# A fixed matmul order through the attention stages of a fused encoder layer, and forget gates summed by a scan

## The chip, the cores and the metric

The kernel runs on one core of a Trainium2 chip. The core has five engines that work side by side, each through its own queue in order: TensorE (PE; matmuls, with a weight load, PEld, ahead of each), VectorE (DVE), ScalarE (ACT), GpSimd (POOL) and SyncE (SP, which here only issues DMAs). They wait for each other through semaphores. The metric is the device time of one execution in microseconds (us), taken as the median of several runs.

## The reference: what is computed

One layer of a streaming encoder on 512 tokens of 1024 channels, all in float32.

- `h = RMSNorm(x)` feeds one input projection of 5640 columns, and four branches take their parts of it: A, differential attention (4 heads, each with two 64-wide halves whose softmaxes are subtracted), F, forgetting attention (8 heads of 64), C, a gated convolution with 31 taps, and D, a short gated convolution with 3 taps.
- Branch F adds a bias to its scores: `c = cumsum(log_sigmoid(f_g + b))` along the tokens, and score `(q, k)` gets `c[q] - c[k]` under a causal mask. `f_g` has 8 columns, one for each head.
- Each branch is projected to 1024 channels and multiplied by `sigmoid(h @ w_gate + b_gate)`; the four are summed and projected once more (`w_out`).
- Then cross-attention into 256 memory tokens, and a gated MLP (2816 wide) with a 3-tap convolution. Each of the three parts is added to the residual after an RMSNorm.

## The kernel before

**Products in three passes.** A float32 number is split into a high part in the engine's fast float32 format and a low part (`split`, `load_weights`), and a product is three matmuls (`mm3`): high by high, high by low, low by high. `load_weights` gives each block of weights a DMA on SP into `wr` (2 buffers), a cast on ACT into `wh` (L129), and a subtraction on DVE into `wl` (L130).

**Blocks.** All the heavy work is a list of jobs. `run_blocks` loads weights two jobs ahead, then runs a job's body and calls `bg.tick()`. A body usually runs `channel_major`: 128 output channels by 512 tokens, summed over 8 slices of the input, 24 matmuls of 512 columns. Its PSUM bank comes from a set of four with the tag `mm`; two more banks have the tag `sc` (attention scores), two the tag `tr` (transposes).

**Background tasks.** Everything else is written as generators held by `bg`. Each `yield cost, wait` gives the step's cost on the other engines and how long the step after it is to be held back. `bg.clock` counts the time of the matmuls emitted so far, 0.42 ns for a column and 0.107 us for a transpose. `tick` spends a credit of 0.7 us for each us of that clock on the first two tasks in the queue, as soon as a task's wait is over. In `channel_major` there is a tick after the fourth of eight slices.

**The attention tasks.** For each A head, `qk_jobs` makes two blocks, q (L490 copies on ACT, L491 subtractions on DVE) and k (L498, L499, L500), into a tile `qk` with 2 buffers; then `a_task` has six steps. Step s (0 to 3) does the scores of 128 queries against (s+1)*128 keys, for both halves, into two `sc` banks; DVE adds the mask and takes the row maximum (L557); ACT takes the exponentials (L562); DVE the reciprocals; ACT scales one half (L566), and DVE subtracts the halves (L567). Step s+1 begins with the transposes of that result (`to_keys_major`), whose split goes to `pt` tiles, and steps 3 and 5 multiply them with v (`values`). `f_task` does the same for a pair of F heads; POOL builds the biases (L718, L720) from rows `ck` and columns `cq` of the cumulative gates.

**Order of the stages.** C blocks, D blocks, gates of D, `v_jobs` (v of branch A), q and k of the four A heads, gates of C, `vf_jobs` (v of branch F and the 8 gate columns), q and k of the F pairs mixed with the gates of A, gates of F (`last_branch_jobs`), `w_out`, cross-attention, MLP. `vf_jobs` ends with `forget_gates`: the 8 columns of all tokens go through 9 small DVE and 2 small ACT operations (L647 to L659), then through matmuls with a triangle of ones (L669, `tri`, built by POOL), which sum along the tokens; ACT scales the sums (L670), POOL writes them to DRAM (`crows`, read back by `f_task` as `ck`), and four transposes of 8 rows make `cq`.

**Who sets the order on an engine.** The program is given to a scheduler, which puts the instructions on each engine by the order in which they were emitted and by its own model of when each is ready. On TensorE, a matmul that is emitted early but not ready by that model is passed by later ones that are ready. What it puts in a queue stays in that order on the chip.

## Time and profile before

| | us |
|---|---|
| median of three runs (1113.37 to 1114.11) | 1113.88 |
| the profiled execution's own time | 1114.43 |
| span of its trace, first to last instruction | 1112.7 |
| PE busy in the span | 1093.3 |
| DVE busy | 690.7 |
| ACT busy | 465.6 |
| POOL busy | 107.0 |

By the trace the attention of branch A lies at about 224 to 330 us, the gates of branch C end at about 366 us, the v products of branch F and the forget gates lie at 366 to 407 us, the attention of branch F at 400 to 545 us, the cross-attention at 640 to 760 us, and the MLP fills the rest.

How to read the lines: the page's part 1 gives each engine's busy time; part 2 cuts the span in 40 slices and gives the busy share of each in tenths, with the clock that TensorE was granted (`PEclk`). Groups and waits name an engine, the tile that it writes and a line of the kernel (`PE ps_tr L170` is a transpose); after an arrow stands what released it. A table by windows gives the busy time of each engine in a stretch of time, with the number of its instructions in brackets. Matmuls are pipelined: one of 512 columns is shown with 0.39 us, but the next starts 0.231 us after it, so TensorE can be shown as busy while it waits a little.

### The profile page before, as it was taken

How to read it: one execution, taken by the hardware profiler on the slowest of the kernel's cores; microseconds unless marked ns; L12 is line 12 of the kernel's file. 1: busy time of each engine (PE TensorE's matmuls, PEld its weight loads, DVE VectorE, ACT ScalarE, POOL GpSimd, SP SyncE). 2: the span in 40 equal slices, each digit the busy share in tenths (PEclk: the TensorE clock that was granted, in tenths of full speed). 3: DMA queues.
4: the chain of work that ended last, by engine and by line, in shares of the span. 5: the costliest groups of instructions: out<-in, count | busy, mean ns of one | idle time of the engine just before them, and what ended most of it. 6: DMA issues, size and time to landing. Idle time of an engine off the chain costs nothing.

```text
span 1112.7 us, 14146 instructions
## 1 busy us (share of the span) xinstructions
PE 1093.3 (98%) x5419; PEld 913.1 (82%) x5419; DVE 690.7 (62%) x1123; ACT 465.6 (42%) x783; POOL 107.0 (10%) x199
## 2 busy tenths in 40 slices
PE   7999999999999999999999999999999999999997
PEld 6888888887878978888888889888888888888886
DVE  4899985457565357766464477677666666642224
ACT  4322222467564255555443255445444444431112
POOL 4000001000101024323010130120000000000001
PEclk9999999999999999999999999999999999999999
DMA  6433432331212233333252252333333333332222
GB/s 188 112 92 96 106 90 88 94 95 57 76 59 77 77 115 95 95 95 85 87 189 96 94 171 96 95 95 106 97 97 97 95 96 95 95 95 95 95 76 76
DMA packets 147896, 109.29 MB, mean 98 GB/s; under 512 B 3647, under 2 KB 135340, under 8 KB 147829
## 3 DMA queue, kind: packets, MB, share of 16 engines
q1 hardware_dynamic: 145269, 99.85, 30.2%
q0 software_dynamic: 2560, 8.54, 2.8%
q8 instruction: 43, 0.70, 0.3%
q14 instruction: 24, 0.20, 0.1%
HBM read 106.27 MB, written 2.11 MB: 97 GB/s over the span
## 4 chain that ended last, share of the span: by engine, by line
PE 92%; DVE 2%; DMA 2%; ACT 1%; issue 1%; POOL 1%; SPq 0%; POOLq 0%; DVEq 0%; ACTq 0%
PE ps_mm L166 80%; PE ps_sc L166 7%; PE ps_tr L166 3%; PE ps_tr L170 3%; DVE wl L130 1%; DMA wr<-in_w_in 1%; DMA wr<-in_w_xo 1%; POOL st_r L195 1%; DVE res L890 1%; ACT wh L129 0%; DMA wr<-in_w_xkv 0%; DMA wr<-in_w_xq 0%; DVE htl L110 0%; PE ps_sc L669 0%; DVE e L557 0%
## 5 line engine op out<-in xcount | busy, mean ns | idle before, releaser
L166 PE MATMUL ps_mm<-hth,wh 128*128 128x512 f32 (+1 forms) x984 | 373.1, 380 | 3.0 <-ACT hth L109 1.7
L166 PE MATMUL ps_mm<-htl,wh 128*128 128x512 f32 (+1 forms) x984 | 372.5, 379 | 0.3 <-DVE htl L110 0.3
L166 PE MATMUL ps_mm<-hth,wl 128*128 128x512 f32 (+1 forms) x984 | 372.2, 379 | 0.0
L130 DVE TENSOR_TENSOR wl<-wr,wh 128x1024 fp32r<-128x1024 f32 (+1 forms) x180 | 221.2, 1230 | 235.5 <-ACT wh L129 231.9
L129 ACT CAST wh<-wr 128x1024 fp32r<-128x1024 f32 (+1 forms) x182 | 190.9, 1049 | 374.8 <-PE ps_mm L166 225.8
L166 PEld LDWEIGHTS ps_mm<-hth,wh 128*128 128x128 f32 x984 | 185.7, 189 | 37.5 <-ACT hth L109 1.9
L166 PEld LDWEIGHTS ps_mm<-htl,wh 128*128 128x128 f32 x984 | 185.9, 189 | 35.0 <-DVE htl L110 0.5
L166 PEld LDWEIGHTS ps_mm<-hth,wl 128*128 128x128 f32 x984 | 185.5, 189 | 35.2 <-issue 0.2
L393 DVE SCALAR_TENSOR_TENSOR y<-y,par,y 128x482 f32<-128x482 f32 (+25 forms) x120 | 82.6, 730 | 0.2
L166 PE MATMUL ps_mm<-y,wh 128*128 128x512 f32 x256 | 80.9, 395 | 0.0
L330 DVE SCALAR_TENSOR_TENSOR c<-ps_mm,par,c 128x510 f32<-128x510 f32 x84 | 62.7, 746 | 1.4
L166 PEld LDWEIGHTS ps_mm<-y,wh 128*128 128x128 f32 x256 | 47.5, 188 | 9.9
L166 PE MATMUL ps_mm<-y,wl 128*128 128x512 f32 x128 | 50.8, 397 | 0.0
L192 POOL TENSOR_SCALAR st_m<-pm 128x1 f32<-128x1 f32 x12 | 2.6, 219 | 459.2 <-ACT junk L1142 349.1
L109 ACT CAST acth<-c 128x512 fp32r<-128x512 f32 x22 | 13.6, 620 | 54.7 <-DVE c L1089 54.7
L718 POOL TENSOR_SCALAR fbias<-ck,cq 128x128 f32<-128x128 f32 (+3 forms) x32 | 29.0, 909 | 70.7 <-DVE st L724 65.9
L166 PE MATMUL ps_mm<-wh,actl 128*128 128x512 f32 x88 | 34.6, 393 | 0.0
L166 PE MATMUL ps_mm<-wl,acth 128*128 128x512 f32 x88 | 34.6, 393 | 0.0
L166 PE MATMUL ps_mm<-wh,acth 128*128 128x512 f32 x88 | 34.2, 392 | 0.0
L1083 ACT ACTIVATE c<-ps_mm,par 128x512 f32<-128x512 f32 x42 | 32.4, 772 | 0.0
L109 ACT CAST pth<-ps_tr 128x512 fp32r<-128x512 f32 (+3 forms) x56 | 23.5, 450 | 20.5 <-PE ps_tr L170 19.5
L166 PE MATMUL ps_sc<-qk 128*128 128x128 f32 (+3 forms) x128 | 29.9, 331 | 1.0 <-DVE st L557 0.9
(268 smaller groups left out, 1574.7 us busy)
## 6 DMA issues: line engine op xcount, KB each, us to landing
wr<-in_w_up SPq DMA_DIRECT2D x44, 512.0 KB
wr<-in_w_in SPq DMA_DIRECT2D x40, 512.0 KB
wr<-in_w_gate SPq DMA_DIRECT2D x32, 512.0 KB
wr<-in_w_down SPq DMA_DIRECT2D x22, 512.0 KB
wr<-in_w_branch SPq DMA_DIRECT2D x16, 512.0 KB
wr<-in_w_out SPq DMA_DIRECT2D x8, 512.0 KB
wr<-in_w_xkv SPq DMA_DIRECT2D x8, 512.0 KB
wr<-in_w_in SPq DMA_DIRECT2D x4, 520.0 KB
```

Source lines behind the costliest of these rows:

```text
L109: A.copy(hi, ps)
L129: A.copy(hi[:, :n], raw[:, :n])
L130: low.tensor_tensor(lo[:, :n], raw[:, :n], hi[:, :n].bitcast(F32), ALU.subtract)
L166: PE.matmul(ps, lhs, rhs, start=start, stop=stop)
L170: PE.transpose(ps, x, ident[:n, :n])
L192: G.tensor_scalar(m, parts[0], EPS, None, ALU.add)
L195: G.tensor_tensor(r, m, nhalf[:, :n], ALU.pow)
L330: V.scalar_tensor_tensor(dst[:, s:], src[:, :S - s], w(k), dst[:, s:], ALU.mult, ALU.add)
L393: V.scalar_tensor_tensor(dst[:, s:], src[:, :S - s], pc("conv_dw", k * 4 + j), dst[:, s:], ALU.mult, ALU.add)
L718: G.tensor_scalar(bias[:, :w], ck[j][:, :w], -1.0, cq[:, qt, head:head + 1], ALU.mult, ALU.add)
L890: V.scalar_tensor_tensor(ns.out[t], scaled, rstd_of(ns.work, ms), src, ALU.mult, ALU.add)
L1083: A.activation(c[:, i], ps, AF.Identity, bias=pc("fb", ch), scale=pc("fdw2", ch))
```

## The change

- In the stages from `v_jobs` to the end of branch F's attention (`keep_order(True)` to `keep_order(False)`), every matmul and every transpose is tied to the one emitted before it (`in_order`), so that TensorE runs them in the emitted order.
- `channel_major` calls `bg.tick()` after each slice but the last, no longer only after the fourth. The clock counts 0.45 ns a column and 0.109 us a transpose. After a step that emitted work on TensorE, no task but the bulk ones (the convolution) may start another step for 1.5 us (`gap`, `free`). Both attention tasks get an extra wait at their start, and each step its own wait in place of one for all.
- The gates' sum: the 8 gate columns are transposed (four transposes into an `sc` bank), ACT scales them, and DVE sums them along the 512 tokens with `tensor_tensor_scan` on 8 partitions. The triangle and its matmuls go.
- The first two gate blocks of branch F's output are emitted ahead of `drain("f")`, no longer behind it.

```diff
-    def __init__(self, rate, width):
+    def __init__(self, rate, width, gap):
...
     def step(self, task):
+        start = self.clock
...
         task[2] = self.clock + wait
+        if self.clock > start:
+            self.free = self.clock + self.gap
         return cost
...
-            while self.credit > 0 and task in self.queue and task[2] <= self.clock:
+            while (self.credit > 0 and task in self.queue
+                   and max(task[2], 0.0 if task[3] else self.free) <= self.clock):
                 self.credit -= self.step(task)
...
-    bg = Background(0.7, 2)
+    bg = Background(0.7, 2, 1.5)
...
+    pe_order = SimpleNamespace(kept=False, last=None)
+
+    def in_order(ins):
+        if pe_order.kept and pe_order.last is not None:
+            tc.add_manual_dep(ins.ins, pe_order.last.name,
+                              mybir.DependencyInfo(mybir.DependencyClass.NoSync, mybir.DependencyReason.DATA),
+                              reason="the order of the tensor engine")
+        pe_order.last = ins.ins
+
+    def keep_order(kept):
+        return None, None, lambda: setattr(pe_order, "kept", kept)
+
     def matmul(ps, lhs, rhs, start, stop):
-        PE.matmul(ps, lhs, rhs, start=start, stop=stop)
-        bg.clock += max(int(math.prod(rhs.shape[1:])), 256) * 0.00042
+        in_order(PE.matmul(ps, lhs, rhs, start=start, stop=stop))
+        bg.clock += max(int(math.prod(rhs.shape[1:])), 256) * 0.00045
...
     def transpose(ps, x, n=P):
-        PE.transpose(ps, x, ident[:n, :n])
-        bg.clock += 0.107
+        in_order(PE.transpose(ps, x, ident[:n, :n]))
+        bg.clock += 0.109
...
-            if k == 3 < nk - 1:
+            if k < nk - 1:
                 bg.tick()
...
     def a_task(h, qk, v):
         es, pt, av = {}, None, None
+        yield 0.0, 4.0
...
-            yield cost, 3.5
+            yield cost, (5.0, 5.5, 6.5, 7.5, 3.0, 2.0)[step]
...
-        tri = m1p.tile([P, S], F32, tag="fbias", name="tri", bufs=2)
-        G.memset(tri, 1.0)
-        G.affine_select(out=tri, in_=tri, pattern=[[1, S]], compare_op=ALU.is_ge, fill=0.0, base=0,
-                        channel_multiplier=-1)
         row = e4()
-        pc_ = bank("sc")
+        rz = e4()
+        G.memset(rz[:8, 1], 1.0)
+        pz = bank("sc")
         for kt in range(NT):
-            n = S - kt * P
-            PE.matmul(pc_[:8, kt * P:], z[:, kt], tri[:, :n], start=kt == 0, stop=kt == NT - 1)
-        A.mul(row[:8, 0], pc_[:8, :], HD ** 0.5)
+            transpose(pz[:8, kt * P:(kt + 1) * P], z[:, kt])
+        A.mul(rz[:8, 0], pz[:8, :], HD ** 0.5)
+        V.tensor_tensor_scan(row[:8, 0], rz[:8, 1], rz[:8, 0], 0.0, ALU.mult, ALU.add)
         G.dma_start(crows, row[:8, 0])
...
     def f_task(p, qk, v):
         f_steps[p] = 0
+        yield 0.0, 3.0
...
-            yield cost, 4.5
+            yield cost, (5.0, 5.5, 6.3, 7.2, 2.5, 2.0)[step]
...
+    gf = gate_blocks(1, "f", lambda m: split(acc[m], ns.mix[0][:, m], ns.mix[1][:, m], 0.5))
+
     def mixer_jobs():
...
         yield then(lambda: y.pop("d"))
+        yield keep_order(True)
         yield from v_jobs(O_AV, va)
...
+        yield from itertools.islice(gf, 2)
         yield then(lambda: bg.drain("f"))
+        yield keep_order(False)
...
     def last_branch_jobs():
         yield then(open_last_branch)
-        yield from gate_blocks(1, "f", lambda m: split(acc[m], ns.mix[0][:, m], ns.mix[1][:, m], 0.5))
+        yield from gf
```

More of the change, by code (lines that the diff above doesn't have):

```diff
@@ L8 @@
+import itertools
 import math
@@ L44, with add @@
 class Background:
-    def __init__(self, rate, width):
-        self.queue, self.rate, self.width = [], rate, width
-        self.clock = self.last = self.credit = 0.0
-    def add(self, gen, name):
-        self.queue.append([name, gen, 0.0])
+    def __init__(self, rate, width, gap):
+        self.queue, self.rate, self.width, self.gap = [], rate, width, gap
+        self.clock = self.last = self.credit = self.free = 0.0
+    def add(self, gen, name, bulk=False):
+        self.queue.append([name, gen, 0.0, bulk])
     def step(self, task):
+        start = self.clock
         try:
@@ L345, in done @@
             V.scalar_tensor_tensor(conv_u[:, j], e[:, 1], 1.0, e[:, 0], ALU.add, ALU.mult)
-            bg.add(conv_task(j), "conv")
+            bg.add(conv_task(j), "conv", True)
         for i in range(8):
```

## The prediction

> **What bounds the kernel now.** The page comes first: busy shares, slices, and the chain that ended last.

> ```profile
> PE 1093.3 (98%) x5419; PEld 913.1 (82%) x5419; DVE 690.7 (62%) x1123; ACT 465.6 (42%) x783; POOL 107.0 (10%) x199
> ...
> PE   7999999999999999999999999999999999999997
> ...
> PEclk9999999999999999999999999999999999999999
> ...
> PE 92%; DVE 2%; DMA 2%; ACT 1%; issue 1%; POOL 1%; SPq 0%; POOLq 0%; DVEq 0%; ACTq 0%
> ```

> TensorE is the bound, so the change can gain only what TensorE loses between matmuls, and it loses whatever it makes TensorE wait. A busy share hides short losses. I therefore went through TensorE's order and gave each matmul the spacing of its kind from the timeline (0.231 us for 512 columns, 0.175, 0.118 and 0.066 for 384, 256 and 128, 0.109 for a transpose), and compared with the clock. 20 to 224 us: nothing lost. 224 to 330 (attention A): 106.0 us for 96.8 us of work, 9.2 lost. 330 to 400: 0.7. 400 to 545 (attention F, the same kinds of steps): 2.8. 640 to 760 (cross-attention): 5.9. The rest: nothing. The windows show the same from outside:

> ```profile
> core 0: us, PE busy (x) PEld busy (x) DVE busy (x) ACT busy (x) POOL busy (x), PEclk, DMA share, GB/s
> 224.00:330.00 106.00, 102.86 (x495) 83.60 (x494) 69.72 (x179) 64.74 (x139) 6.04 (x10) 0.98 0.25 73
> 400.00:545.00 145.00, 145.00 (x733) 120.69 (x732) 95.54 (x221) 77.60 (x160) 45.95 (x79) 1.00 0.32 96
> 250.00:253.39 3.39, 2.00 (x11) 1.27 (x11) 3.35 (x13) 1.63 (x5) 0.00 (x0) 1.00 0.09 14
> 253.39:256.80 3.41, 3.41 (x11) 2.36 (x11) 2.96 (x11) 3.39 (x13) 1.04 (x2) 0.50 0.42 142
> 256.80:260.00 3.20, 3.20 (x15) 2.60 (x14) 2.60 (x6) 2.47 (x6) 0.00 (x0) 1.00 0.00 0
> ```

> The reader is to see 3.1 us of open idle time in A and none in F, and that 1.39 us of idle time (250 to 253.39) was followed by 3.41 us at half the granted clock, in which 512-column matmuls start 0.425 us apart. F's loss, 2.1 us without the gates' part, is the floor of such steps; scaled to 106 us it is 1.5. So order and spacing can win back at most 9.2 - 1.5 = 7.6 us.

> The third view is the timeline of DVE and ACT around the forget gates. TensorE's last v matmul started at 388.55, and TensorE went straight on with the next block:

> ```profile
> 390.27 0.42 DVE L110 TENSOR_TENSOR v<-ps_mm,v 128x256 fp32r<-128x256 f32 x1
> ...
> 392.54 0.19 DVE L647 TENSOR_TENSOR fz<-fz_raw,bfg 128x32 f32<-128x32 f32 x1
> ...
> 395.95 0.19 DVE L659 TENSOR_TENSOR fz<-fz,fd 128x32 f32<-128x32 f32 x1
> ...
> 389.89 1.05 ACT L129 CAST wh<-wr 128x1024 fp32r<-128x1024 f32 x1
> ...
> 393.24 1.28 ACT L652 ACT_TABLE_LOAD   x1
> ...
> 402.07 0.59 ACT L670 ACTIVATE e<-ps_sc 8x512 f32<-8x512 f32 x1 [1.21 <-PE ps_sc L669]
> ...
> 399.38 0.40 PE L166 MATMUL ps_mm<-htl,wh 128*128 128x512 f32 x1
> 399.71 2.32 PE L669 MATMUL ps_sc<-tri,fz 128*8 128x512 f32 x8
> 401.96 0.51 PE L166 MATMUL ps_mm<-hth,wl 128*128 128x512 f32 x1
> ```

> The chain through the gates took 3.60 us (392.54 to 396.14), and TensorE did other work for 11 us before it read the result.

> **The change, part by part.**

> *Forget gates.* Before, the eight triangle matmuls held TensorE from 399.61, where the next block matmul was due, to 401.96, plus 0.12 on the matmul behind them; the four row transposes took 0.43 (406.90 to 407.56, less 0.23): 2.9 us. Now both groups of transposes are emitted directly behind the last v matmul, and the order is kept. In the built order of the changed kernel nothing stands between: v matmul, four transposes of the gates, four of the summed rows, then the first q block of branch F. TensorE waits for the whole chain. From the start of the last v matmul: its result at 0.28; on ACT the copy of the third v bank, then a weight cast that is released by that last matmul (1.05), then the last copy (0.37); on DVE the weight subtraction that needs the cast (1.23), the last v subtraction and the gate columns' copy, to 3.1; the chain 3.6, to 6.7; transposes 0.1 + 3 x 0.109 + 0.27, to 7.4; ACT's scale with a hop 0.65, to 8.1; the scan; a hop and the four row transposes 0.45. No row shows a scan. Operations on 512 columns took 0.48 (L733) to 0.75 (L567), twice the dearest would be 1.5; I take 0.75, the row with two tensor inputs. First block matmul at 9.4, in place of 0.12: 9.3 lost (8.3 if the cast and subtraction do not stand in front, 10.5 at the long ends). Net 9.3 - 2.9 = **+6.4** (5.4 to 7.6). Behind the waiting transposes stands all of TensorE's queue, and behind it every engine.
> [...]

> *The clock after that pause.* Six of those 9.3 us are without a matmul, more than the 1.39 that was followed by half clock. In 3.41 us at half clock, 3.41 x (1 - 0.231/0.425) = 1.6 us is lost. Nothing (the half clock falls into the pause) to 3.1 (two such stretches); I take **+1.6**.
> [...]

> *Attention A.* The 7.6 go, and new waits come. By the built order I counted TensorE's work between a step's scores and the transposes of its result: 5.5 to 8.5 us. Against this stands the chain of the step with what the queues of ACT and DVE put before it. Head 0, second step: spacing 5.54; a cast that TensorE releases 1.4 after the scores (1.05), two exponentials 1.4, two k copies 1.2, L566 0.5, L567 0.48: 6.0, late by 0.5. Head 0, last step: spacing 8.2; two q copies, a cast, four k copies, a split, four exponentials, L566 and L567 add up by their rows to 9.5, and with a hop that is late by 1.4. Head 1, last step: all four `mm` banks are held, and the gate block after the next 6 matmuls (1.4) needs the bank that a tanh empties; ACT has a q copy, two k copies, a cast and the tanh in front, 3.5: late by 2.2. Head 2: 0.3 and 0.1. The others arrive in time. Sum 4.5. Bounds: 0, as all chains alone (3.3 to 5.2 by their rows) fit; and 9.3, if each chain takes the time that the same step took before, leaving out the three in which DVE's first operation waited 9 to 10 us for a buffer. For the 2.2 us wait I add half of a half-clock stretch, 0.8 (none followed a 1.37 us wait at 660 us). -7.6 + 4.5 + 0.8 = **-2.3**.

> *Attention F.* Spacing 5.54 to 10.2; the same chains took 3.1 to 7.0 before (4.6 to 6.0 at 5.54, 4.9 to 6.2 at 7.67, 5.5 to 7.0 at 7.2 and 7.6). POOL's biases start as soon as the step before has read its own, 5 us ahead; `crows` is written 9 us after the v products but `ck` is first read 16 us of matmuls later, and the round trip took 6.9 (402.95 to 409.82). **+0.3** (0 to 2).

> *At nothing:* more ticks in the convolution stage, because TensorE lost nothing there and its order is the same up to the v blocks; cover gone, DVE (90% busy in slices 2 to 4) would delay bank evictions. The two early gate blocks, because TensorE lost nothing at that seam. POOL's triangle, 10% busy. Cross-attention: nearly the same order, its waits stay (±1). SP's queue: same loads, same order.

> Sum: 1114.43 + 6.4 + 1.6 - 2.3 + 0.3 = 1120.4 in the profiled execution's terms; that one was 0.55 above its median, so **1119.9**.

> **The rivals.**
> 1. *All of A's waits vanish (not slower).* The steps never queue behind a cast, and the clock stays up after the pause: 1113.9 + 6.4 - 7.6 + 0.3 = 1113.0. It decides once A gives back over 6.7 us with no half clock. For it: chains alone fit their spacing. Against: the built queues put casts and copies between.
> 2. *A's chains stay as slow as before:* waits of 9.3 and 2 in F: 1113.9 + 6.4 + 1.6 + 1.7 + 2 = 1125.6. Against: a minimum gap of 1.5 us between steps thins the queues.
> 3. *The clock returns late:* two half-clock stretches behind the pause, 1121.4. [...]
> 4. *The pause does not come:* block matmuls pass the waiting transposes. Then 1113.9 - 2.0 - 2.3 = 1109.6. Against: the built order, which an engine's queue keeps.

> **How the numbers follow.** Forecast 0.62, rivals 0.13, 0.12, 0.10, 0.03. Most likely 1119.9. Leaving out the far halves of rivals 1 and 2 and rival 4 gives 1114.5 to 1125. About 0.2% is what a measurement can tell from no change (1111.7 to 1116.1): slower 0.84, same 0.11 (most of rival 1), faster 0.05.

> **What would show it.** Right: one idle stretch of TensorE of 8 to 10 us around 375 to 395 us, before `ps_sc` and `ps_tr` transposes and released by DVE (fz, then the scan's `e`); a granted clock of 0.5 right after it; in A single waits of 1 to 2.5 us, released by ACT's tanh and by L567's successor; none over 0.5 us in F. Wrong: block matmuls between the two groups of transposes, or A's loss under 2 us.

## The result and the profile after

| | before | after |
|---|---|---|
| median, us | 1113.62 (1111.03 to 1114.11, 4 runs) | 1129.66 (1128.45 to 1132.51, 4 runs) |
| profiled execution, us | 1114.43 | 1130.0 |
| span of its trace, us | 1112.7 | 1128.2 |

The changed kernel takes 1.0151 times as long, 95% interval 1.0138 to 1.0164. It is slower, as forecast, but by 16 us and not by 6, and beyond the range.

The page of the changed kernel, busy shares, slices and the chain's shares by engine:

```profile
PE 1095.0 (97%) x5415; PEld 916.2 (81%) x5415; DVE 692.4 (61%) x1124; ACT 465.0 (41%) x783; POOL 98.4 (9%) x198
...
PE   7999999999999799999999999989999999999997
...
PEclk9999999999999989999999999999999999999999
...
PE 90%; DVE 3%; DMA 3%; ACT 2%; issue 1%; POOL 1%; SPq 0%; POOLq 0%; DVEq 0%; ACTq 0%
```

Two dents are new in the slices of PE: the 14th slice (367 to 395 us, the forget gates) and the 27th (733 to 762 us, the end of the cross-attention). The prediction put the second one at nothing (±1 us). The waits of TensorE in the changed kernel name both:

```profile
PE ps_sc L189 <- DVE fz L679: 7.7, 1, 7.7
PE ps_mm L185 <- ACT wh L135: 3.9, 3, 2.2
...
PE ps_mm L185 <- ACT ge L778: 2.1, 1, 2.1
PE ps_sc L185 <- ACT hth L115: 2.0, 2, 1.8
PE ps_tr L189 <- DVE e L688: 1.9, 1, 1.9
...
PE ps_mm L185 <- DVE ge L790: 0.9, 1, 0.9
PE ps_mm L185 <- DVE vxl L116: 0.9, 1, 0.9
PE ps_tr L189 <- DVE xe L1004: 0.7, 1, 0.7
```

The columns are the total wait, how often, and the longest one, in us; the long waits among the lines left out stand in the kernel before too. The 7.7 and the 1.9 are the pause at the gates. The 2.1 at L778 is the gate block in A that waits for a tanh. The long ones of `wh` (2.2) and `hth` (1.8) lie at 749 to 752 us, where the cross-attention hands over to the MLP; this document calls such a boundary between two stages a seam.

I counted lost time by stage in the way of the prediction (the clock's time less the spacing of the matmuls issued in it):

| stage | lost before | lost after |
|---|---|---|
| A | 9.2 | 7.0 |
| v blocks of F and gates (before 378 to 412 us; after the same, with 1.7 us less spacing because the triangle went) | 0.9 | 13.6 |
| attention F, 412 to 545 us | 2.1 | 3.3 |
| cross-attention and first up blocks, 640 to 780 us | 6.1 | 11.2 |
| everything else, nearly all of it in the first 20 us | 9.1 | 9.7 |

The losses grow by 17.4 us, the spacing falls by 1.7 us: 15.7, against 15.6 between the two profiled executions. The losses hold the time lost at half clock too: one stretch of 3.41 us in A in either profile, and in the changed kernel's four behind the gates and one behind the cross-attention.

**The gates.** The timeline of the changed kernel around the pause, lines of DVE, ACT and PE:

```profile
387.04 1.23 DVE L136 TENSOR_TENSOR wl<-wr,wh 128x1024 fp32r<-128x1024 f32 x1 [3.57 <-ACT wh L135]
...
389.25 1.21 DVE L136 TENSOR_TENSOR wl<-wr,wh 128x1024 fp32r<-128x1024 f32 x1
...
390.90 0.19 DVE L667 TENSOR_TENSOR fz<-fz_raw,bfg 128x32 f32<-128x32 f32 x1
...
394.31 0.19 DVE L679 TENSOR_TENSOR fz<-fz,fd 128x32 f32<-128x32 f32 x1
396.23 1.21 DVE L688 TENSOR_TENSOR_SCAN e<-e 8x512 f32<-8x512 f32 x1 [1.73 <-ACT e L687]
...
395.61 0.59 ACT L687 ACTIVATE e<-ps_sc 8x512 f32<-8x512 f32 x1 [2.49 <-PE ps_sc L189]
...
386.56 0.28 PE L185 MATMUL ps_mm<-wh,htl 128*128 128x264 f32 x1
394.56 1.01 PE L189 MATMUL ps_sc<-ident,fz 128*8 128x128 f32 x4 [7.72 <-DVE fz L679]
397.50 0.59 PE L189 MATMUL ps_tr<-ident,e 8*128 8x8 f32 x4 [1.93 <-DVE e L688]
398.02 0.79 PE L185 MATMUL ps_mm<-hth,wh 128*128 128x512 f32 x1
```

From the start of the last v matmul to the first block matmul it is 398.02 - 386.56 = 11.46 us. Two weight subtractions stand on DVE ahead of the gates' chain, where the prediction had one, and the scan took 1.21 us.

The windows of the changed kernel around and behind the pause (from and to, length, PE, PEld, DVE, ACT and POOL busy, the granted clock, DMA share, GB/s):

```profile
386.91:390.32 3.41, 0.00 (x0) 0.00 (x0) 3.28 (x6) 2.13 (x6) 0.00 (x0) 1.00 0.12 33
390.32:393.73 3.41, 0.00 (x0) 0.00 (x0) 1.80 (x11) 1.74 (x3) 0.00 (x0) 0.50 0.83 239
393.73:397.15 3.42, 1.01 (x4) 0.35 (x4) 1.63 (x5) 0.59 (x1) 0.00 (x0) 0.50 0.12 36
397.15:400.56 3.41, 3.06 (x10) 2.55 (x11) 0.48 (x2) 0.00 (x0) 1.28 (x3) 0.50 0.03 5
400.56:403.97 3.41, 3.41 (x9) 2.64 (x9) 0.00 (x0) 0.00 (x0) 0.71 (x2) 0.50 0.45 154
403.97:407.38 3.41, 3.41 (x16) 2.75 (x16) 0.00 (x0) 1.01 (x2) 1.07 (x4) 1.00 0.00 0
```

The clock is halved for four stretches, 13.65 us, of which six us lie behind the pause: from 398.02 to 404.32 us, 6.30 us were spent on 15 matmuls, 3.46 us of spacing; 2.8 lost.

**The seam from the cross-attention to the MLP.** First the kernel before, then the changed one; lines of PE and ACT from the timelines:

```profile
733.66 1.04 PE L170 MATMUL ps_tr<-ident,nt 128*128 128x128 f32 x8
...
737.08 0.28 PE L166 MATMUL ps_sc<-hth,wh 128*128 128x256 f32 x1
...
738.17 0.38 PE L166 MATMUL ps_sc<-htl,wh 128*128 128x256 f32 x1 [0.69 <-DVE htl L110]
```

```profile
746.79 1.04 PE L189 MATMUL ps_tr<-ident,nt 128*128 128x128 f32 x8
749.60 0.39 PE L185 MATMUL ps_sc<-hth,wh 128*128 128x256 f32 x1 [1.76 <-ACT hth L115]
...
752.43 0.58 PE L185 MATMUL ps_mm<-hth,wh 128*128 128x256 f32 x1 [2.22 <-ACT wh L135]
...
748.97 1.06 ACT L115 CAST hth<-ps_tr 128x512 fp32r<-128x512 f32 x2
751.33 1.04 ACT L135 CAST wh<-wr 128x1024 fp32r<-128x1024 f32 x1 [1.30 <-DMA wr<-in_w_up]
```

Before, the transposes of the normed tokens (`nt`) stand in the midst of the last output-projection matmuls, 3.4 us ahead of the first up block. After, they stand behind the last of them, and the first up block needs their split at once: TensorE waits 1.76 us. The scheduler then put the first matmul of each of four up blocks ahead of everything else, and the fourth has to wait for its weights, 2.22 us. A stretch at half clock (752.13 to 755.55 us, granted 0.50) follows.

### The profile page after: what moved, and what is told of

It reads as the page before. It is cut to its first block, busy times and chain, and to the rows that moved or that the text cites. A ratio compares the mean times of both kernels' runs of the same rounds, so it can differ in the third digit from the quotient of the medians.

```text
span 1128.2 us, 14142 instructions
## 1 busy us (share of the span) xinstructions
PE 1095.0 (97%) x5415; PEld 916.2 (81%) x5415; DVE 692.4 (61%) x1124; ACT 465.0 (41%) x783; POOL 98.4 (9%) x198
## 4 chain that ended last, share of the span: by engine, by line
PE 90%; DVE 3%; DMA 3%; ACT 2%; issue 1%; POOL 1%; SPq 0%; POOLq 0%; DVEq 0%; ACTq 0%
PE ps_mm L185 78%; PE ps_sc L185 7%; PE ps_tr L189 3%; PE ps_tr L185 3%; DVE wl L136 1%; DMA wr<-in_w_in 1%; ACT wh L135 1%; POOL st_r L214 0%; DMA wr<-in_w_xkv 0%; DMA wr<-in_w_xq 0%; DVE res L914 0%; DMA wr<-in_w_up 0%; DMA wr<-in_w_xo 0%; DVE htl L116 0%; DVE qk L519 0%
## 5 line engine op out<-in xcount | busy, mean ns | idle before, releaser
L116 DVE TENSOR_TENSOR ptl<-ps_tr,pth 128x512 fp32r<-128x512 f32 (+3 forms) x56 | 28.6, 515 | 13.5 <-ACT pth L115 13.1
L185 PE MATMUL ps_mm<-wh,hth 128*128 128x256 f32 (+1 forms) x96 | 30.8, 321 | 0.0
```

What stands on the lines that cost most here:

```text
L116: V.tensor_tensor(lo, ps, hi.bitcast(F32), ALU.subtract)
L185: in_order(PE.matmul(ps, lhs, rhs, start=start, stop=stop))
```

## The experiments

All ratios are to the kernel before on the same chip: 1114.0 (17 runs), 1113.47 (17 runs) and 1113.93 (16 runs) in the three groups. The losses by stage are those of one profiled execution of each kernel. None of these kernels leaves out a part of the computation.

**Where the seam's loss comes from.** The gap holds for every task but the bulk ones, and so for the norm's transposes at the seam, which have nothing to do with attention.

```diff
-    bg = Background(0.7, 2, 1.5)
+    bg = Background(0.7, 2, 0.0)
...
-        return None, None, lambda: setattr(pe_order, "kept", kept)
+        return None, None, lambda: (setattr(pe_order, "kept", kept), setattr(bg, "gap", 1.5 if kept else 0.0))
```

> The changed kernel with the 1.5 us minimum gap between steps counted only while the order is kept; everything else stays. Theory G (the gap pushes the last norm transposes of the cross-attention behind the last output-projection matmuls, so that the first up blocks wait 1.9 + 2.4 us for their splits and a half-clock stretch follows): the loss between 640 and 780 us falls from 11.2 to about 6 us, no half-clock stretch there, and the kernel takes about 1124.5 us, 5 less than the changed one. Rival T (the ticks after every slice, or the faster clock, moved them): the loss and the time stay, 1129 to 1130.

Measured: 1125.20 us (1124.3 to 1127.3), ratio 1.0106 (1.0091 to 1.0121), 4.5 less than the changed kernel. The loss from 640 to 780 us fell from 11.2 to 7.6. The timeline of PE at the seam:

```profile
744.98 1.03 PE L189 MATMUL ps_tr<-ident,nt 128*128 128x128 f32 x8
...
747.48 0.28 PE L185 MATMUL ps_sc<-hth,wh 128*128 128x256 f32 x1
...
748.56 0.39 PE L185 MATMUL ps_sc<-htl,wh 128*128 128x256 f32 x1 [0.68 <-DVE htl L116]
```

The transposes are back among the projection's matmuls and the two long waits and the half clock are gone (the matmuls of 256 columns from 748.79 us start 0.12 us apart, in the changed kernel 0.21 from 752.81 us): theory G holds, with 3.6 of the 5.1 us. The 1.5 us that stay (7.6 against 6.1) are waits at 715 to 719 us (`vxl` and `xe`, in the changed kernel too); they are gone in the kernels that have the ticks and the clock's rates of before in this stage (below, 5.9). Between the two profiled executions there are 5.1 us; some 1.7 of them lie at the gates, where the clock was halved for three stretches and not four, so the gap does not explain all of the 4.5.

**Where the pause comes from.**

```diff
-                forget_gates(dst[1])
+                kept, last = pe_order.kept, pe_order.last
+                pe_order.kept = False
+                forget_gates(dst[1])
+                pe_order.kept, pe_order.last = kept, last
```

> The changed kernel with the forget gates' eight transposes left out of the kept order, so that block matmuls may pass them. Theory P (the pause is TensorE in order behind the gates' chain): the waits of 7.9 and 2.2 us and the 13.65 us at half clock go, the loss around the gates falls from 13.6 to under 1, and the kernel takes 1116 to 1117.5 us. Rival S (the scan's chain itself is late for branch F, which reads its rows): a part of the pause comes back as waits at the first scores of F or before its biases, 1119 or more.

Measured: 1121.18 us (1118.5 to 1124.5), ratio 1.0066 (1.0051 to 1.0081), 8.5 less than the changed kernel. In its profiled execution (1118.48) the pause and the four stretches at half clock are gone (granted clock 0.995 over the execution, 0.988 in the changed kernel), and the stage loses 4.0 in place of 13.6. So the order makes the pause: theory P. But theory P had under 1 us left, and 1116 to 1117.5. The profiled execution is the fastest of the six: of the 11.5 us between it and the changed kernel's, 9.6 are the gates, and most of the rest is a half-clock stretch that A had there and not here. Two waits of the changed kernel's order come out from behind the pause, as the waits of this kernel show:

```profile
PE ps_mm L185 <- DVE v L116: 1.6, 1, 1.6
...
PE ps_tr L189 <- DVE e L755: 1.2, 1, 1.2
```

The first block of F waits for a bank that a v copy empties, and the first step of F waits for its result. The granted clock of its six runs went from 0.991 to 0.996, and the slowest run has the lowest, but the range of 6 us follows it only in part.

**Wait or clock.** 28 matmuls fill most of the pause, so that less of it is idle.

```diff
+        pd = bank("sc")
+        for i in range(28):
+            matmul(pd, ht[0][:, i % 8, :P], ht[0][:, i % 8, :], True, True)
         pz = bank("sc")
```

> The changed kernel with 28 matmuls of 512 columns on ready data put ahead of the first four transposes of the gates (6.5 us of work whose result nobody reads), so that TensorE works through most of the 7.9 us wait. Theory C (3.5 of the 13.6 us lost there are the half clock after the pause, not the wait): the clock stays at full speed or is halved for one stretch of 3.41 us, and the kernel is 1.9 to 3.5 us faster, 1126 to 1128. Rival W (the 13.6 us are waits, the half clock falls in them): the time stays within 0.5 us, or grows if the matmuls hold the transposes up.

Measured: 1127.85 us (1127.1 to 1130.7), ratio 1.0130 (1.0117 to 1.0143), 1.8 less; its profiled execution is the slowest of the four (1130.67). In that one two stretches at half clock follow and not four, from 394.22 to 401.05 us:

```profile
390.81:394.22 3.41, 0.66 (x5) 0.27 (x4) 1.93 (x7) 0.59 (x1) 0.00 (x0) 1.00 0.30 91
394.22:397.63 3.41, 2.86 (x10) 2.35 (x11) 0.69 (x2) 0.00 (x0) 1.07 (x2) 0.50 0.03 5
397.63:401.05 3.42, 3.42 (x10) 2.65 (x9) 0.00 (x0) 0.00 (x0) 0.66 (x2) 0.50 0.49 152
```

The loss on the work behind the pause is still 2.7 us (changed kernel: 2.8). Counting the fill as lost time, since nobody reads its result, the stage lost 13.1 in place of 13.6. Neither theory is confirmed: the fill shortens the half clock where it would have fallen into the pause anyway, and the two waits that stay (1.4 and 1.9 us) leave TensorE 2.75 us without work in one stretch, behind which the clock is halved. Where the rest of the 1.8 us lies is open, and the profile cannot tell: its granted clock is 0.992 where the changed kernel's is 0.988, and the cross-attention lost some 3.5 us more, with a wait of 2.8 us for weights.

**The scan by itself**, in the kernel before, with the order left to the scheduler (the diff is the one of the gates' sum).

> The kernel before with the scan in place of the triangle and nothing else, the order left to the scheduler. If the scan is worth what its matmuls held TensorE (2.15 us of spacing less 0.44 for four transposes, with block matmuls passing its chain): 1.7 to 2 us faster than before, 1111.6 to 1112.2. If the scan's longer chain is late for branch F's biases: no gain, or slower than before.

Measured: 1112.53 us (1111.0 to 1113.4), ratio 0.9987 (0.9979 to 0.9996), 1.5 less than before, a little short of the 1.7 to 2. The scan takes 1.21 us there too, and TensorE has no wait over 0.4 us in that stage. As a part the scan is a small gain; with the kept order it stands in the pause.

**Order and spacing apart.** Four kernels have the scan, and in branch A alone (from `v_jobs` to the end of the A steps) the order, the spacing (gap, ticks, rates and the steps' waits), or both; the fourth has both from there to the end of F, with the gates left out of the order. The first three have the early gate blocks of F at their old place, the fourth at the new one.

```diff
-        return None, None, lambda: setattr(pe_order, "kept", kept)
+            pe_order.kept, pe_order.spaced = kept, spaced
+            bg.gap = 1.5 if spaced else 0.0
...
-            if k < nk - 1:
+            if k < nk - 1 and (k == 3 or pe_order.spaced):
...
-            yield cost, (5.0, 5.5, 6.5, 7.5, 3.0, 2.0)[step]
+            yield cost, (5.0, 5.5, 6.5, 7.5, 3.0, 2.0)[step] if pe_order.spaced else 3.5
...
+        yield keep_order(False, False)
         yield from vf_jobs(vf)
```

> The kernel before with the scan, and the kept order, the gap, the ticks, the clock's rates and the steps' own waits only in branch A (from its v blocks to the end of its steps); forget gates, branch F and all later stages as before. Theory O (the order pays in A and nowhere else): A's loss falls from the 9.1 us of the scan alone to the 5.4 to 7.0 of the changed kernel, and the time from 1112.5 to 1108.8 to 1110.4. Rival: what A gives back is lost again at its seams, 1112 or more.

> The same with the kept order in A alone, the steps issued as before (wait of 3.5 us, no gap, a tick after the fourth slice). If the order alone pays, 1109 to 1110.5. If TensorE in order then waits for each chain (5 to 7 us against spacings that begin at 3.5), A's loss grows by 0.5 to 1 us for each of some 16 steps: 1117 or more.

> The same with the spacing in A alone (gap, ticks, rates, waits), the order left to the scheduler. If the spacing pays, 1109 to 1110.5. If the scheduler moves the steps by its own model whatever the spacing, within 0.7 us of 1112.5.

> The changed kernel with the forget gates left out of the kept order, and gap, ticks and rates of the clock as before outside the kept stages. From the losses by stage: the changed kernel's 1129.7 less 9.6 (gates 13.6 to 4.0) and 5.1 (cross-attention 11.2 to 6.1) is 1115.0, range 1113.5 to 1116.5. Against the kernel with the order in A alone this shows what the order costs in F and at the seam before it: theory O has 4 to 6 us. If the order pays in F too, it is as fast as the other.

| in A | time, us | ratio to before | lost in A |
|---|---|---|---|
| neither (scan alone) | 1112.53 | 0.9987 (0.9979 to 0.9996) | 9.1 |
| order | 1124.17 | 1.0100 (1.0087 to 1.0113) | 20.8 |
| spacing | 1108.35 | 0.9961 (0.9948 to 0.9974) | 5.6 |
| order and spacing | 1108.58 | 0.9962 (0.9950 to 0.9974) | 5.4 |
| both, and both in F | 1114.15 | 1.0007 (0.9999 to 1.0016) | 5.4 |

The first row was measured beside the first group (before: 1114.0), the others beside the second (1113.47), so the ratios are what compares. Theory O falls. The spacing gives all of A's gain without the order; the order adds nothing to it, and alone it costs some 12 us. From 224 to 330 us the granted clock was 0.98 in the first and third row and 0.95 in the second: the losses in A hold one half-clock stretch there, and three. The fifth row, with 0.999 over its whole execution (some 2.2 us at half clock), has room for none. The same spacing without such a stretch lost 4.3 us (the kernel with spacing in A and F, below, 0.999 too), so the order even costs A some 1 us: with it TensorE waits 2.1 us for the tanh, without it 0.7. The medians do not show that difference.

Where the order alone loses its 12 us, the waits of that kernel show:

```profile
PE ps_sc L188 <- ACT qk L521: 5.5, 4, 2.1
PE ps_sc L188 <- DVE qk L522: 2.6, 4, 1.2
...
PE ps_sc L188 <- DVE st L580: 2.1, 3, 0.7
PE ps_tr L192 <- DVE e L590: 2.0, 3, 0.7
```

A step issued right behind its k block has TensorE in order wait for the copies of q and k. Left to the scheduler, block matmuls pass such a step: the kernel with the scan alone has no wait for `qk` over 0.3 us. The fifth row, within the 1113.5 to 1116.5 expected, has the order's price in F and at the seam before it, 5.6 us; the spacing in F is not it (below), and the early gate blocks were not tried by themselves. Its profiled execution (1111.5) is near the lowest of twelve and only 2.9 above the profiled one of the fourth row: it lost 2.6 more at the v blocks and gates, among it 1.2 at the first transposes of F, and 1.2 more in F, with one wait of 0.9 us for `ge`, and less at the start. The rest of the 5.6 I could not place. Its cross-attention loses 5.9, about as before (6.1).

**What of the spacing pays.** The kernel with the spacing alone, once without the gap, once with the old waits, and once with the spacing also in F.

```diff
-            bg.gap = 1.5 if spaced else 0.0
+            bg.gap = 0.0
```

```diff
-        yield 0.0, 4.0 if pe_order.spaced else 0.0
...
-            yield cost, (5.0, 5.5, 6.5, 7.5, 3.0, 2.0)[step] if pe_order.spaced else 3.5
+            yield cost, 3.5
```

> The kernel with the spacing in branch A alone (1108.4, order left to the scheduler), without its 1.5 us gap; the steps' own waits and the ticks stay. If the waits of 5 to 7.5 us are what pays, within 0.7 us of 1108.4. If the gap pays by keeping two tasks from issuing together, back towards 1112.5.

> The same kernel with the gap and the ticks, but with the wait of 3.5 us after every step and none at a task's start, as before. If the waits pay, back towards 1112.5 (more if steps come in faster with the added ticks). If the gap pays, within 0.7 us of 1108.4.

> The same spacing in branch A and from the v products of F to the end of F's steps, the order left to the scheduler throughout. F lost 2.1 to 2.3 us with the old spacing, no more than a floor, so spacing should gain nothing there: 1108.4 within 0.7. If the 1.2 us that F loses more in the changed kernel come from the spacing and not from the order, 1109.5 or more.

Measured: 1113.43 us without the gap (ratio 0.9999, 0.9991 to 1.0008; A loses 9.2), 1116.57 with the old waits (1.0027, 1.0015 to 1.0038; A loses 13.0), 1108.42 with spacing in A and F (0.9959, 0.9945 to 0.9972; F loses 2.2). Both parts of the spacing are needed: either without the other gives nothing, or costs some 4 us; the ticks and the clock's rates were not tried by themselves. And F's extra 1.2 us in the changed kernel come with the order: the same spacing without it loses 2.2 there, as before, and the wait of 0.9 us for `ge` is gone.

The kernel with the scan and the spacing in A alone beats both kernels: 1108.35 us, 0.9961 of the time before (0.9948 to 0.9974).

## Why the prediction was wrong, point by point

- **"At nothing: ... Cross-attention: nearly the same order, its waits stay (±1)": this step failed,** by the most: +5.1 us. I had gone by which instructions stand in the stage, and had left out the one group that moved by a few matmuls, the norm's transposes ahead of the up blocks. The gap, a rule in a planner that all tasks share, moved it, and the cover that I had not named (3.4 us of projection matmuls) was gone. The run that counts the gap in the kept stages alone shows this for 3.6 of the 5.1 us; the other 1.5 are waits at 715 to 719 us that are gone where the ticks and the clock's rates are as before.
- **"Forget gates", the pause: right in kind, too small.** Forecast 9.4 us from the last v matmul to the first block matmul, measured 11.46, outside the 10.5 of the long ends. Two weight subtractions stood ahead of the chain where I had one (+1.2); the scan took 1.21 and not 0.75 (+0.5); the first transposes ran at half clock, 1.05 us to ACT's start where I had 0.7 (+0.35). The chain itself took 3.6 us as before. (The terms as listed add up to 9.3 and not 9.4; in A, 9.2 less 1.5 is 7.7 and not 7.6. Neither matters.) The 0.75 for the scan was the row of another operation (L567); no row of before showed a scan.
- **"The clock after that pause": mis-sized.** Forecast 1.6 us (0 to 3.1), measured 2.8 on the work behind the pause. The half clock did not begin with the end of the idle time and last for one stretch; it began at 390.32 us, within the pause, and lasted until 403.97, 6 us after the first block matmul. That is rival 3, nearly at its price (two stretches, 3.1); in the profile of before the stretches at 14.46 and 253.39 us had stood alone. The stretch from 397.15, which has 0.35 us of idle time and four small transposes, was followed by another at half clock (0.50 from 400.56), and that one, with no idle time, by full clock (1.00 from 403.97).
- **"Attention A": the size was right** (forecast -2.3, measured -2.2), with the wait for the tanh at 2.1 as forecast at 2.2 and the half clock behind it. Part of that is luck: the same wait was followed by half clock in the changed kernel (0.50 from 284.51 us) and not in the one with the gates left out of the order (1.00 from 283.92 us), and the two kernels of the table with this order and spacing lost 5.4 us in A and not 7.0; and the next longest wait in A was 0.6 where 1.4 was forecast. The reason was not right: I gave the -7.6 to "order and spacing", and the runs show that spacing alone does it.
- **"Attention F": +0.3 forecast, +1.2 measured,** inside its bounds. I expected no single wait over 0.5 us, and one of 0.9 came (`ge`, where a projection matmul waits for a bank that a gate block still holds).
- The other rivals: A's waits did not vanish (1), nor did its chains stay as slow as before (2), and the pause came (4).

Added up: 2.1 us of the miss from the pause, 1.2 from the clock behind it, 5.1 from the cross-attention, 0.9 from F; some 9.3 of the 9.8 us between forecast and median. The kernel with the gates out of the order and the rules of before outside the kept stages (fifth row) is back at 1114.15 us, 1.0007 of the time before.

## What to carry to other kernels

Keeping an engine's order is only as good as the emitted order: before it is fixed, every instruction that is emitted right behind its producer has to be found, because each turns into the latency of its whole chain (here 11.5 us for eight tiny transposes), while room between dependent steps helped in A with or without the order (20.8 to 5.4 us lost with it, 9.1 to 5.6 without), and gained nothing in F, where little was lost (2.1 us before, 2.2 with it). A rule put into a planner that other stages share has to be costed in each of those stages, at the places where a stage ends and its cover runs out.

## What was unexpected of the hardware

```profile
281.09:284.51 3.42, 1.35 (x6) 0.83 (x5) 3.35 (x7) 3.36 (x6) 0.87 (x2) 1.00 0.00 0
284.51:287.92 3.41, 3.41 (x11) 2.73 (x11) 1.77 (x5) 3.32 (x8) 0.00 (x0) 0.50 0.45 121
```

```profile
280.51:283.92 3.41, 1.53 (x7) 0.93 (x5) 3.34 (x9) 3.13 (x5) 1.04 (x2) 1.00 0.00 0
283.92:287.33 3.41, 3.21 (x16) 2.67 (x17) 1.89 (x4) 3.32 (x8) 0.00 (x0) 1.00 0.31 83
```

2.07 us of idle time in one window of the grid, and the next is halved; 1.88, with the rest of the wait in the neighbouring window, and it is not. Between 200 and 800 us of the profiles of before and after, three windows of the grid began at full clock and had 2.07 us or more of idle time (2.07 from 281.09 us, 3.41 from 386.91, 2.79 from 748.72, all after), and each was followed by one at half clock; so was the 2.75 us of the kernel with the fill. With less, both happened: in the kernel before, 1.39 us of idle time (249.98 to 253.39) was followed by half clock and 1.37 us (659.58 to 662.99) was not, nor was the 1.88 us here. Idle time in the window alone does not tell these cases apart.
